# Eight fixed PSUM banks in rings, in place of banks that the framework hands out

## The chip, the cores and the metric

The kernel runs on one core of one Trainium2 chip. The metric is device time in microseconds. The unchanged kernel takes 2862.86 us, the median of three runs (2862.85 to 2863.44). TensorE (PE) multiplies matrices and writes the sums to PSUM, a memory of 8 banks; a bank holds 128 partitions of 512 fp32 numbers, one tile of this kernel. VectorE (DVE) and ScalarE (ACT) read the sums out. A bank may be written again only when its reader is done.

## The reference

The reference computes one step of a two-layer encoder trunk for 1024 frames of a new stream and 32 frames of a running one, width 1024, all in fp32:

```
for layer in range(2):
    h = rmsnorm(x, norm_w[layer])
    x = x + (ssd_mixer(h) if layer == 0 else hgrn_mixer(h))
    x = x + (silu(hn @ w_gate) * (hn @ w_up)) @ w_down      # hn = rmsnorm(x), hidden width 2816
y = rmsnorm(x, final_norm_w)
```

`ssd_mixer` projects to 5152 columns, runs a causal convolution of four taps over 3072 of them and a chunked state-space scan of 32 heads, gates and normalizes the result and projects back. `hgrn_mixer` projects to 4 x 1024, runs a chunked gated linear recurrence of 8 heads of 128 x 128, and projects back. States and the convolution's last rows are outputs too.

## The kernel before

The frames stand in the free dimension and are worked on in two halves: half 0 has 512 frames and half 1 has 512 + 32, which matmuls take in two blocks of 272. Features stand on the partitions, so a product of a 128-column piece of a weight with a half needs 8 steps of 128 for the width 1024. An fp32 product is made of three faster ones: each operand is split into a high part (a copy on ScalarE in a shorter format, `wh`, `fh`, `xn`) and the rest (a subtraction on VectorE, `wl`, `fl`), and `product` issues high x high (L344), high x low (L345) and low x high (L346) into one PSUM tile.

The work runs in this order: statistic and normalization of x; the SSD projections, convolution and scan, both halves; its output projection; FFN 1, half 0 then half 1; the HGRN mixer; FFN 2; the final norm. Four groups of products matter here:

- `psum_mm` tiles hold dense products: the projections, the FFN's gate, up and down products. `psum_sc` tiles hold the rest: transposes, the small products of the scans, and the sum over features of a norm's statistic (`rstd_of`, L367 and L365).
- The FFN's hidden units are made partly by `ffn_unit`, which combines inputs and weights before multiplying so that fewer products are needed (`part`, L1103 to L1105), with tiles `px`, `py`, `pz`. `ffn_outs` then multiplies a slab of hidden units by the down weights (an "out") and `accumulate` has VectorE add each result to the running sum, a fixed tile (`fixed<-mm,fixed` in the profile).
- In the SSD mixer, `ssd_cols` transposes the packed time steps `dt` four times for a half (L540), each followed by a copy on VectorE (L541).
- In the HGRN mixer, each of 16 head units runs chunks: a score product (L884), two transposes (L888, L889) that ScalarE copies to `hkv`, a state product (L899) and an output product (L901, L903).
- `last_outs` is the last stretch: the down products of the last two slabs of FFN 2, half 1 (L1381), with the final norm between them. Its tiles come from `psum_mm((0, 1))`.

Many functions are lifted: the framework's scheduler sets the order of instructions on each engine from priorities and data dependencies, among them when a PSUM tile is free. Before the change a product asks the pool `pm` for a tile by a tag, `mm0` to `mm4` or `sc`. In the built program tiles of every tag lie in all eight banks: the framework assigns them.

## Time and profile before

| | |
|---|---|
| median of 3 runs | 2862.86 us |
| the profiled execution's own time | 2863.26 us |
| its span (first to last instruction) | 2861.5 us |
| busy: TensorE, VectorE, ScalarE | 2830.7, 2139.4, 1571.6 us |
| mean granted TensorE clock | 0.999 |
| matmuls in the profile | 19676 |

A group's busy time is the sum of its durations; matmuls are pipelined, so one that is shown with 0.40 us follows the one before after 0.23 us. "idle before <-releaser" in a row of the timeline is the time in which its engine had nothing to do, and what ended it. A window's row lists, after its length, the busy time of TensorE, of its weight loads, of VectorE, ScalarE and GpSimd, each with its count, then the granted clock, the share of DMA time and GB/s.

### The profile page before, as it was taken

The numbers are of one execution on the slowest core, as the hardware profiler recorded it, in microseconds if no ns is written. First come the engines' busy times: TensorE is split into PE (matmuls) and PEld (weight loads), VectorE is DVE, ScalarE is ACT, GpSimd is POOL, SyncE is SP. The second block draws the span as 40 slices with busy tenths as digits, with TensorE's granted clock in tenths as the row PEclk, the third lists the DMA queues.
The fourth block names the chain that finished last, engine by engine and source line by source line (L and its number), as shares of the span: only waits on it lengthen the run. The fifth ranks groups of instructions, "written<-read, shape, count | busy, mean of one in ns | idle before, by whom it ended". The sixth has DMA issues, their size and how long they took to land.

```text
span 2861.5 us, 48969 instructions
## 1 busy us (share of the span) xinstructions
PE 2830.7 (99%) x19676; PEld 2608.2 (91%) x19676; DVE 2139.4 (75%) x3712; ACT 1571.6 (55%) x2926; POOL 40.8 (1%) x157
## 2 busy tenths in 40 slices
PE   8999999999999999999999999999999999999998
PEld 7777788999979999999999888999988999999998
DVE  7887887787787877797777566556658877787776
ACT  6665654564644644465444567656544644455544
POOL 0000000000100000000000000000000000000000
PEclk9999999999999999999999999999999999999999
DMA  6443334444322332323333222222222332333322
GB/s 183 114 114 110 95 101 111 115 112 106 104 79 89 118 103 91 111 90 97 96 97 105 59 76 83 79 80 73 80 83 89 119 96 89 120 93 109 109 91 69
DMA packets 394518, 281.56 MB, mean 98 GB/s; under 512 B 16289, under 2 KB 382514, under 8 KB 394290
## 3 DMA queue, kind: packets, MB, share of 16 engines
q1 hardware_dynamic: 394274, 278.42, 33.5%
q8 instruction: 154, 2.52, 0.4%
q14 instruction: 74, 0.61, 0.1%
q10 hardware_dynamic: 16, 0.00, 0.0%
HBM read 270.57 MB, written 7.82 MB: 97 GB/s over the span
## 4 chain that ended last, share of the span: by engine, by line
PE 91%; DVE 5%; ACT 2%; issue 1%; DMA 0%; SPq 0%; POOL 0%; DVEq 0%; ACTq 0%; POOLq 0%
PE mm L344 18%; PE mm L345 18%; PE mm L346 18%; PE mm L1105 5%; PE mm L1103 5%; PE mm L1104 5%; PE sc L1105 4%; PE sc L1104 4%; PE sc L1103 4%; PE sc L659 1%; PE sc L648 1%; PE sc L645 1%; PE mm L1381 1%; DVE fixed L116 1%; DVE ca L119 1%
## 5 line engine op out<-in xcount | busy, mean ns | idle before, releaser
L113 ACT ACTIVATE wh<-raw 128x512 fp32r<-128x512 f32 (+1 forms) x687 | 555.1, 817 | 616.5 <-PE mm L345 510.5
L344 PE MATMUL mm<-xn,wh 128*128 128x272 f32 (+2 forms) x1552 | 523.3, 338 | 5.1 <-ACT wh L113 2.1
L346 PE MATMUL mm<-xn,wl 128*128 128x272 f32 (+2 forms) x1552 | 517.9, 334 | 1.7 <-DVE wl L116 1.7
L345 PE MATMUL mm<-xn,wh 128*128 128x272 f32 (+2 forms) x1552 | 516.9, 333 | 0.0
L116 DVE TENSOR_TENSOR wl<-raw,wh 128x1024 fp32r<-128x1024 f32 (+1 forms) x307 | 372.6, 1216 | 80.2 <-ACT wh L113 61.0
L116 DVE TENSOR_TENSOR fixed<-mm,fixed 128x272 f32<-128x272 f32 (+3 forms) x504 | 259.0, 524 | 193.1 <-PE mm L346 186.6
L344 PEld LDWEIGHTS mm<-xn,wh 128*128 128x128 f32 x1552 | 291.6, 188 | 35.4 <-ACT wh L113 3.1
L344 PE MATMUL mm<-fh,wh 128*128 128x272 f32 (+1 forms) x992 | 322.5, 327 | 0.3 <-ACT fh L113 0.3
L345 PE MATMUL mm<-fl,wh 128*128 128x272 f32 (+1 forms) x992 | 322.5, 326 | 0.0
L346 PE MATMUL mm<-fh,wl 128*128 128x272 f32 (+1 forms) x992 | 322.4, 326 | 0.0
L346 PEld LDWEIGHTS mm<-xn,wl 128*128 128x128 f32 x1552 | 291.6, 188 | 30.4 <-DVE wl L116 2.1
L345 PEld LDWEIGHTS mm<-xn,wh 128*128 128x128 f32 x1552 | 292.0, 188 | 27.2 <-issue 1.0
L116 DVE TENSOR_TENSOR wh<-raw,wh 128x512 fp32r<-128x512 f32 x380 | 255.6, 684 | 39.8 <-ACT wh L113 36.9
L1103 PE MATMUL mm<-th,wh 128*128 128x272 f32 (+1 forms) x912 | 260.7, 286 | 0.7 <-ACT s L113 0.7
L1105 PE MATMUL mm<-th,wh 128*128 128x272 f32 (+1 forms) x912 | 259.9, 285 | 0.2 <-DVE wh L116 0.2
L1104 PE MATMUL mm<-tl,wh 128*128 128x272 f32 (+1 forms) x912 | 259.7, 285 | 0.0
L344 PEld LDWEIGHTS mm<-fh,wh 128*128 128x128 f32 x992 | 186.2, 188 | 16.9 <-ACT fh L113 1.9
L346 PEld LDWEIGHTS mm<-fh,wl 128*128 128x128 f32 x992 | 186.6, 188 | 15.5
L345 PEld LDWEIGHTS mm<-fl,wh 128*128 128x128 f32 x992 | 186.6, 188 | 15.0 <-DVE fl L116 0.2
L1103 PEld LDWEIGHTS mm<-th,wh 128*128 128x128 f32 x912 | 171.8, 188 | 2.5 <-ACT s L113 1.8
L1104 PE MATMUL sc<-xn,wh 128*128 128x272 f32 (+1 forms) x608 | 173.3, 285 | 0.0
L1103 PE MATMUL sc<-xn,wh 128*128 128x272 f32 (+1 forms) x608 | 172.9, 284 | 0.0
(289 smaller groups left out, 6712.9 us busy)
## 6 DMA issues: line engine op xcount, KB each, us to landing
raw<-in_ffn_w_gate_dram SPq DMA_DIRECT2D x88, 512.0 KB, 3.8
raw<-in_ffn_w_up_dram SPq DMA_DIRECT2D x88, 512.0 KB, 3.9
raw<-in_ffn_w_down_dram SPq DMA_DIRECT2D x88, 512.0 KB, 3.5
raw<-in_ssd_in_w_dram SPq DMA_DIRECT2D x80, 512.0 KB, 4.0
raw<-in_hgrn_in_w_dram SPq DMA_DIRECT2D x64, 512.0 KB, 4.2
cumB<-cumd SPq DMA_DIRECT2D x64, 256.0 KB, 5.3
raw<-in_ssd_out_w_dram SPq DMA_DIRECT2D x32, 512.0 KB, 5.3
raw<-in_hgrn_out_w_dram SPq DMA_DIRECT2D x16, 512.0 KB, 3.8
```

The source lines that it names most:

```text
L113: keep(A.activation(out=out, in_=in_, func=f, **kw))
L116: keep((eng or V).tensor_tensor(out=out, in0=a, in1=b, op=op))
L119: keep(V.scalar_tensor_tensor(out=out, in0=a, scalar=s, in1=b, op0=op0, op1=op1))
L344: PE.matmul(ps[:, :bn], a, mh, start=(k == 0), stop=False)
L345: PE.matmul(ps[:, :bn], a, ml, start=False, stop=False)
L346: PE.matmul(ps[:, :bn], b, mh, start=False, stop=(k == n - 1))
L645: PE.matmul(y23[:, j, :n], S[:, j * P:(j + 1) * P], Cx, start=True, stop=True)
L648: PE.matmul(pp, Btok[:n, :], xw[:n, :], start=True, stop=True)
L659: PE.matmul(y13[r:r + 64, i // 2, :n], xdt[:n, i * 64:(i + 1) * 64], cums[i // 4][:n, i % 4, :n], start=True, stop=True)
L1103: PE.matmul(ps[:, :n], a, mh, start=(k == 0 and not more), stop=False, skip_group_check=True)
L1104: PE.matmul(ps[:, :n], a, ml, start=False, stop=False, skip_group_check=True)
L1105: PE.matmul(ps[:, :n], b, mh, start=False, stop=(k == 3), skip_group_check=True)
```

## The change

Eight PSUM tiles are made once, one for each bank, and kept: `mm0` to `mm3` in banks 0 to 3 and `sc4` to `sc7` in banks 4 to 7. Every kind of product has a tuple of banks, and each tuple has a counter that moves by one with each request in the order in which the code is issued. Dense products take 0, 1, 2, 3; scans, transposes and statistics 4, 5, 6, 7; the FFN's outs, the final norm's transposes and the statistics inside an FFN half take 2, 3, 4; `px` takes 0, 1 as before, `py` and `pz` 5, 6, 7; `last_outs` 0, 1. The three matmuls, the copies, the DMAs and their numbers stay. Lines of the profile after the change lie 3 later up to about line 1008 and 6 later behind it (L344 becomes L347, L1381 becomes L1387).

```diff
-    turn = [0]
-
-    def psum_mm(among=(0, 1, 2, 3, 4)):
-        turn[0] += 1
-        i = among[turn[0] % len(among)]
-        return pm.tile([P, 512], F32, tag=f"mm{i}", bufs=1, name=nm("mm"))
+    banks = [pm.tile([P, 512], F32, tag=f"bank{i}", bufs=1, name=f"{'mm' if i < 4 else 'sc'}{i}") for i in range(8)]
+    turns = {}
+
+    def psum(among):
+        turns[among] = turns.get(among, -1) + 1
+        return banks[among[turns[among] % len(among)]]
+
+    def psum_mm(among=(0, 1, 2, 3)):
+        return psum(among)
 
     def psum_sc():
-        return pm.tile([P, 512], F32, tag="sc", bufs=3, name=nm("sc"))
+        return psum((4, 5, 6, 7))
...
-    def rstd_of(tiles, blocks, scale, width, keep=None, halves=False):
+    def rstd_of(tiles, blocks, scale, width, keep=None, halves=False, bank=psum_sc):
...
-            ps = psum_sc()
+            ps = bank()
...
+    def psum_outs():
+        return psum((2, 3, 4))
...
-        py, pz = psum_sc(), psum_sc()
+        py, pz = psum((5, 6, 7)), psum((5, 6, 7))
...
-            ps = psum_mm((2, 3, 4))
+            ps = psum_outs()
             product(ps, ws[c], (m * P) % cols, hid, b0, bn)
             accumulate(h, m, ps, b0, bn)
...
-        due = ffn_half(layer, 0, xn[0], tx[0], HEAD, lambda: r.append(x_stat(1, st[2])), [2])
+        due = ffn_half(layer, 0, xn[0], tx[0], HEAD, lambda: r.append(x_stat(1, st[2], psum_outs)), [2])
```

Three places of TensorE's order show what this moves. A row is a line, an operation, the tile it writes, the tiles it reads and the shape; before, every request has a tile of its own with a number of its own, while after the change the name is the bank.

The tail, `last_outs`, before: the first three products of the last slabs, `mm_4776`, `mm_4777` and `mm_4778`, and the last product of an FFN unit, `mm_4741`, between them.

```order
L1381 MATMUL mm_4776_30752<-fh_4733_30505,wh_4766_30732 128x288
...
L1105 MATMUL mm_4741_30552<-th_4275_26916,wh_4757_30698 128x272
L1381 MATMUL mm_4776_30752<-fl_4736_30511,wh_4766_30732 128x288
L1381 MATMUL mm_4776_30752<-fh_4735_30510,wl_4767_30733 128x288
L1381 MATMUL mm_4777_30760<-fh_4733_30505,wh_4766_30732 128x288
...
L1381 MATMUL mm_4778_30768<-fh_4733_30505,wh_4766_30732 128x288
```

The same rows after:

```order
L1387 MATMUL mm0_72<-fh_3164_28944,wh_3194_29168 128x288
...
L1111 MATMUL mm1_73<-th_2842_25491,wh_3185_29134 128x272
L1387 MATMUL mm0_72<-fl_3167_28950,wh_3194_29168 128x288
L1387 MATMUL mm0_72<-fh_3166_28949,wl_3195_29169 128x288
L1387 MATMUL mm1_73<-fh_3164_28944,wh_3194_29168 128x288
...
L1387 MATMUL mm0_72<-fh_3164_28944,wh_3194_29168 128x288
```

Nothing has moved; the third product now writes the bank of the first.

The outs of the first slabs of FFN 1, half 0, about 840 us into the span, before: the last matmuls of the SSD output projection, the statistic (L367) between transposes of the final SSD state (L584), and the first matmul of each of five outs.

```order
L346 MATMUL mm_1439_8941<-xn_92,wl_1437_8913 128x512
L584 MATMUL sc_1441_8971<-fixed_72 128x128 x4
L584 MATMUL sc_1443_8979<-fixed_72,Ss_1281_7992 128x128
L367 MATMUL sc_1450_9011<-sq_1445_8999,fixed_72 128x272
L584 MATMUL sc_1443_8979<-fixed_72,Ss_1281_7992 128x128 x3
L367 MATMUL sc_1451_9014<-sq_1445_8999,fixed_72 128x272
L344 MATMUL mm_1463_9044<-fh_1409_8784,wh_1461_9040 128x512
...
L344 MATMUL mm_1464_9052<-fh_1409_8784,wh_1461_9040 128x512
...
L344 MATMUL mm_1465_9060<-fh_1409_8784,wh_1461_9040 128x512
...
L344 MATMUL mm_1466_9068<-fh_1409_8784,wh_1461_9040 128x512
...
L344 MATMUL mm_1470_9082<-fh_1409_8784,wh_1468_9078 128x512
```

After:

```order
L370 MATMUL sc5_77<-sq_957_8519,fixed_80 128x272
L370 MATMUL sc6_78<-sq_957_8519,fixed_80 128x272
L348 MATMUL mm2_74<-xn_100,wh_952_8436 128x512
L349 MATMUL mm2_74<-xn_100,wl_953_8437 128x512
L587 MATMUL sc7_79<-fixed_80 128x128 x4
L587 MATMUL sc4_76<-fixed_80,Ss_855_7574 128x128 x4
L347 MATMUL mm3_75<-fh_933_8316,wh_971_8558 128x512
L347 MATMUL mm2_74<-fh_933_8316,wh_971_8558 128x512
...
L347 MATMUL sc4_76<-fh_933_8316,wh_971_8558 128x512
...
L347 MATMUL mm2_74<-fh_933_8316,wh_971_8558 128x512
...
L347 MATMUL mm3_75<-fh_933_8316,wh_974_8592 128x512
```

The statistic now stands ahead of the transposes and of two matmuls of the projection, and the outs go through three banks.

The start of the SSD mixer, some 50 us into the span, before: the end of one convolution product, the first matmul of the next (`mm_82`), and the transposes of dt further on.

```order
L344 MATMUL mm_75_605<-xn_92,wh_71_573 128x256
L345 MATMUL mm_75_605<-xn_92,wh_71_573 128x256
L346 MATMUL mm_75_605<-xn_92,wl_72_574 128x256
L344 MATMUL mm_82_648<-xn_92,wh_79_642 128x256
...
L540 MATMUL sc_96_790<-fixed_72,dt_50_359 128x128
L540 MATMUL sc_97_793<-fixed_72,dt_50_359 128x128
L540 MATMUL sc_98_796<-fixed_72,dt_50_359 128x128
L344 MATMUL mm_107_814<-xn_92,wh_104_809 128x512
```

After:

```order
L347 MATMUL mm2_74<-xn_100,wh_47_557 128x256
L348 MATMUL mm2_74<-xn_100,wh_47_557 128x256
L349 MATMUL mm2_74<-xn_100,wl_48_558 128x256
L543 MATMUL sc7_79<-fixed_80,dt_32_349 128x128
L543 MATMUL sc4_76<-fixed_80,dt_32_349 128x128
L543 MATMUL sc5_77<-fixed_80,dt_32_349 128x128
L543 MATMUL sc6_78<-fixed_80,dt_32_349 128x128
L641 MATMUL sc5_77<-fixed_80,ca_30_341 128x128
L347 MATMUL mm3_75<-xn_100,wh_53_624 128x256
```

The four transposes, 96 rows further on before, stand ahead of the convolution product `mm3` (before, `mm_82`), and behind them a transpose of the first convolved tile, `ca`, into the bank of the third.

More of the change, by code (lines that the diff above doesn't have):

```diff
@@ L1006, in trunk_kernel, with x_stat @@
     NB = 1
-    def x_stat(h, keep):
-        return rstd_of([acc[h][m][:, :LEN[h]] for m in range(KD)], BLK[h], 1.0 / D, LEN[h], keep)
+    def x_stat(h, keep, bank=psum_sc):
+        return rstd_of([acc[h][m][:, :LEN[h]] for m in range(KD)], BLK[h], 1.0 / D, LEN[h], keep, bank=bank)
+    def psum_outs():
+        return psum((2, 3, 4))
     def norm_pieces(h, wc, out, blocks, r, tags=XN, keep=None):
@@ L1288, in mixer_ffn @@
                 dma(wrow[q], final_norm_w[q * 512:(q + 1) * 512].unsqueeze(0).to_broadcast([P, 512]))
-            done = [lambda g=g: finish(g, lambda: psum_mm((2, 3, 4))) for g in groups_of(0, 0, H1)]
-        due = ffn_half(layer, 1, xn[1], tx[1], 1, lambda: r.append(nxt and x_stat(0, st[3])),
+            done = [lambda g=g: finish(g, psum_outs) for g in groups_of(0, 0, H1)]
+        due = ffn_half(layer, 1, xn[1], tx[1], 1, lambda: r.append(nxt and x_stat(0, st[3], psum_outs)),
                        [2] if nxt else [1, 1], done)
@@ L1342, in first @@
             for g, ss in zip(groups, sums):
-                ps, yo = finish_half(g, 0, ss, lambda: psum_mm((2, 3, 4)), "n")
+                ps, yo = finish_half(g, 0, ss, psum_outs, "n")
                 tt(yo[:g[2], :], ps[:g[2], :], wrow[0][:g[2], :], MUL)
```

## The prediction

> **What bounds the kernel now.** I read the page first, then the list of what TensorE waits for, then single stretches of the timeline.
>
> ```profile
> span 2861.5 us, 48969 instructions
> PE 2830.7 (99%) x19676; PEld 2608.2 (91%) x19676; DVE 2139.4 (75%) x3712; ACT 1571.6 (55%) x2926; POOL 40.8 (1%) x157
> PEclk9999999999999999999999999999999999999999
> PE 91%; DVE 5%; ACT 2%; issue 1%; DMA 0%; SPq 0%; POOL 0%; DVEq 0%; ACTq 0%; POOLq 0%
> ```
>
> TensorE is busy 2830.7 of 2861.5 us and makes 91% of the chain of waits. All its idle time is 2861.5 - 2830.7 = 30.8 us, so no arrangement of banks can gain more than that, while a new wait of TensorE goes into the time one for one. The list of its waits (engine, tile and line that waits, then what it waits for; total, times, longest) says which part of the idle time is about banks:
>
> ```profile
> PE mm L210 <- DMA fixed<-in_x_prompt_dram: 4.2, 1, 4.2
> PE sc L899 <- ACT hkv L113: 2.2, 2, 1.2
> PE mm L344 <- DVE fixed L886: 2.0, 2, 1.7
> PE mm L344 <- DVE fixed L116: 1.3, 1, 1.3
> PE mm L344 <- ACT pre L113: 1.3, 2, 0.8
> PE mm L344 <- DVE hq L119: 0.8, 1, 0.8
> ```
>
> A first matmul of a product (L344) that waits for the engine reading an older product waits for its bank: rows three to six, 2.0 + 1.3 + 1.3 + 0.8 = 5.4 us. The others wait for operands. So what banks cost today is about 5.4 us of 2861.5, and what is to be weighed is what three or four banks per kind add.
>
> **The change part by part.** No matmul, copy or DMA is added or removed. Every bank must be emptied by its reader before the ring comes round to it. The cost at a place is the time at which VectorE or ScalarE has read the bank, less the time at which TensorE would write it again; both can be read from the trace wherever the order stays as it is. The order is the same around 850 to 1500, 2100 to 2500 and 2500 us to the end but for a few rows, and differs in the first 165 us, in 350 to 460, 700 to 850 and 1500 to 2110 us.
>
> *The tail* (`last_outs`, L1381). The first rows are TensorE's, the others VectorE's.
>
> ```profile
> 2825.99 0.41 PE L1381 MATMUL mm<-fh,wh 128*128 128x288 f32 x1 [0.26 <-ACT fxd L113]
> 2826.90 0.30 PE L1381 MATMUL mm<-fh,wh 128*128 128x288 f32 x1
> ...
> 2825.81 1.22 DVE L116 TENSOR_TENSOR wl<-raw,wh 128x1024 fp32r<-128x1024 f32 x1
> 2828.78 0.72 DVE L116 TENSOR_TENSOR fl<-fxd,fh 128x544 fp32r<-128x544 f32 x1
> 2829.42 3.00 DVE L116 TENSOR_TENSOR fixed<-mm,fixed 128x288 f32<-128x288 f32 x8
> ```
>
> The second and third of these product groups begin at 2825.99 and 2826.90. VectorE works through low halves of weights (from 2825.81) and of the hidden rows (2828.78) and reaches the first accumulate at 2829.42. Today the groups run on into other banks. With banks 0 and 1 alone the third group writes the bank of the first, so it starts when that accumulate ends, one of eight accumulates later, at 2829.42 + 3.00 / 8 = 2829.8, or a little after: **+3.0 us**. Afterwards a group takes 0.9 us of TensorE (2825.99 to 2826.90) against 0.4 of an accumulate, and nothing more is lost. Nothing behind can hide it: the rest of the span is this chain.
>
> *The first outs of FFN 1* (512 columns, ring of banks 2, 3, 4).
>
> ```profile
> 846.59 0.40 PE L344 MATMUL mm<-fh,wh 128*128 128x512 f32 x1
> ...
> 846.31 2.18 DVE L119 SCALAR_TENSOR_TENSOR Y<-Y,fixed,rstd 128x544 f32<-128x544 f32 x3 [1.28 <-ACT rstd L113]
> 850.37 1.88 DVE L116 TENSOR_TENSOR fixed<-mm,fixed 128x512 f32<-128x512 f32 x3
> ```
>
> The fourth out starts at 846.59. The first three accumulates come at 850.37, behind the gating of the SSD output that VectorE does in order; the first ends a third into them and a little later, at 851.05. With three banks the fourth out waits for it: 851.05 - 846.59 = 4.4 us. The change also puts the statistic that releases VectorE (1.28 us of waiting for `rstd`) some 1.3 us earlier in TensorE's order. VectorE can come earlier by no more than that wait, so the ends are 4.4 - 1.28 = 3.1 and 4.4; I take **+3.2**.
>
> *Three more places of outs.* After slab 4 of the same FFN, and at the head of the second half of each FFN, where VectorE makes the input combinations (`xt`, `tl`) between the accumulates:
>
> ```profile
> 907.61 0.40 PE L344 MATMUL mm<-fh,wh 128*128 128x512 f32 x1
> ...
> 908.70 0.68 DVE L116 TENSOR_TENSOR fixed<-mm,fixed 128x512 f32<-128x512 f32 x1
> ...
> 2506.81 0.29 PE L344 MATMUL mm<-fh,wh 128*128 128x272 f32 x1
> ...
> 2508.01 1.13 DVE L116 TENSOR_TENSOR fixed<-mm,fixed 128x272 f32<-128x272 f32 x3
> 2500.00:2520.00 20.00, 19.84 (x154) 19.29 (x153) 19.08 (x42) 8.43 (x17) 0.00 (x0) 1.00 0.09 27
> ```
>
> The sixth out (907.61) needs the third accumulate (908.70 + 0.68 = 909.38): 1.8, of which I give back 0.8 for short waits that stand there today: **+1.0**. The seventh out at 2506.81 needs the fourth accumulate, first of the three at 2508.01, ended at 2508.44: 1.6, and in the next groups up to 2.1. VectorE is busy 19.08 of these 20 us (third number pair of the row), so it can't catch up: **+1.8**. The same stretch of FFN 1 at 1216 to 1231 us has the same instructions with VectorE a little freer: **+1.3**.
>
> *The start of the SSD mixer.* The four transposes of dt (L540) and a transpose behind them (L638) are moved in front of a convolution product.
>
> ```profile
> 50.45 0.28 PE L344 MATMUL mm<-xn,wh 128*128 128x256 f32 x1
> 59.85 0.38 PE L344 MATMUL mm<-xn,wh 128*128 128x256 f32 x1 [0.79 <-ACT pre L113]
> 65.23 0.33 PE L540 MATMUL sc<-fixed,dt 128*128 128x128 f32 x1 [1.05 <-ACT pre L113]
> ...
> 52.63 0.68 DVE L116 TENSOR_TENSOR dt<-dt,dt 32x512 f32<-32x512 f32 x1
> 53.35 0.75 DVE L119 SCALAR_TENSOR_TENSOR ca<-pre,fixed,ca 128x512 f32<-128x512 f32 x1
> 65.54 0.88 DVE L541 COPY fixed<-sc 128x128 f32<-128x128 f32 x4
> ```
>
> TensorE is at that product at 50.45; dt is ready at 52.63 + 0.68 = 53.31, and the extra transpose writes the bank of the third of the four, whose copy comes after `ca` (53.35 + 0.75) and three copies of 0.22: about 54.8. That is 4.3 us of standing. Queued behind it on TensorE is the convolution product, and behind that ScalarE's `pre`. The waits of 0.79 and 1.05 us at 59.85 and 65.23 go: **+2.4**; ends 0 and 4.3.
>
> *HGRN mixer* (1590 to 2110 us, 16 head units). Its four small products per chunk share banks 4 to 7, and the statistic takes one of them, so that twice in a unit a bank comes round early: the transposes (L888, L889) of the next unit follow the last ones in the same bank with one product and three 512 or 272 wide matmuls between, about 0.7 us from write to write.
>
> ```profile
> 1593.97 0.27 PE L889 MATMUL sc<-fixed,hv 128*128 128x128 f32 x1
> 1594.28 0.39 ACT L113 ACTIVATE hkv<-sc 128x256 f32<-128x256 f32 x1 [0.51 <-PE sc L889]
> 1600.60 0.27 PE L889 MATMUL sc<-fixed,hv 128*128 128x128 f32 x1
> 1602.73 0.37 ACT L113 ACTIVATE hkv<-sc 128x256 f32<-128x256 f32 x1
> ```
>
> The copy that frees the bank is done 1594.28 + 0.39 - 1593.97 = 0.70 us after the write where ScalarE stands ready, and 2.5 us after it where ScalarE is busy (1600.60, 1602.73). So a place costs 0 or up to 1.8. Of 32 places I let a quarter cost half of that, 32 x 0.25 x 0.9 = 7, take back the 2.0 + 0.8 us of L886 and `hq` waits, and one more for places that hide each other: **+3**; ends -5 and +11. Outside the mixer half of the two 1.3 us waits should go: **-1**. The rest of the reordered rows, at the start and in 700 to 835 us, I take as 0, give or take 3, since TensorE's queue there is dense in both orders.
>
> Sum: 3.0 + 3.2 + 1.0 + 1.8 + 1.3 + 2.4 + 3 - 1 = 14.7 us. Against the profiled execution's own 2863.26 us, which lies 0.4 above the median of 2862.86, that is **2878 us**, or +0.5%.
>
> [...]
>
> **The rivals.**
>
> *Gain.* Banks that are free by rule end the bank waits of today, and the new order feeds TensorE better: the statistic at 840 us and the dt transposes already move forward. Of the 30.8 us of idle time 4.2 is the wait for x; if half of the rest goes and the outs hide, only the tail adding its 3.0, it gives 2863.3 - 13.3 + 3.0 = 2853, within 2850 and 2859. Against it: the 5.4 us of bank waits is all that I could find for certain.
>
> *Absorbed.* While TensorE stands, VectorE and ScalarE catch up, so that a stall early on pays for a later one, and only the tail remains, with half of the outs' 7.3 us, less some 3 us of bank waits that go: 3.0 + 3.6 - 3 gives 2867. For it: VectorE has a quarter of the span free. Against it: at 2500 to 2520 it has not.
>
> *Compounding.* The mixer's short turns cost their 11 us and the SSD start is not regained (4.3): 14.7 + 8 + 2 = +25, 2888.
>
> [...]
>
> *The change doesn't do what it says.* The framework might already keep tags to banks, and the rings would then be nearly the old ones. The built order speaks against it: products that the code tags alike lie in all eight banks before. It would give 2863.
>
> **How the numbers follow.** The forecast holds 0.50, compounding 0.13, the clock 0.05, absorbed 0.16, nothing done 0.03, gain 0.13. A measurement of this kernel can tell about 0.2% from no change, 5.7 us: below 2857.1 is faster, above 2868.6 slower. Of the gain rival 0.11 lies below 2857 and 0.02 within; of the absorbed one 0.12 within and 0.04 above; nothing done lies within. So faster has 0.11, no change 0.12 + 0.03 + 0.02 = 0.17, and slower 0.50 + 0.13 + 0.05 + 0.04 = 0.72. The range leaves out one in ten on either side: low 2858, where the gain begins; high 2892, past compounding by the 3 us of the unknown reorderings. The forecast's own range is 2870 to 2886.
>
> **What would show it.** The tail: a wait of the `last_outs` matmuls for VectorE's `fixed` of about 3.0 us, and the first accumulate at the same distance from the end of the product as now. The outs: a wait of `product`'s first matmul for VectorE of about 3 us some 846 us in, and waits of 1 to 2 us near 907, 1220 and 2507. The start: one of the dt transposes waiting about 2.9 us for `dt`, then the extra one 1.4 us for `fixed`. The mixer: transposes into a `sc` bank waiting for ScalarE's `hkv`, ten or so, none above 2 us. [...] I am wrong if the outs and the tail show no wait for VectorE, if VectorE's own order of accumulates is earlier than now, or if the waits are there and the time isn't because as much idle time vanished elsewhere.

## The result

The changed kernel takes 2897.57 us (median of four runs, 2896.24 to 2899.33) against 2863.15 us (2862.85 to 2863.5) for the kernel before: a ratio of 1.0121, with a 95% interval of 1.0103 to 1.0138. It is slower, as forecast, but by 34.4 us and not by 14.7, and outside the range of 2858 to 2892.

The page of the changed kernel, with the rows that answer to those shown of before (its profiled execution took 2899.33 us):

```profile
span 2897.6 us, 48939 instructions
PE 2846.6 (98%) x19676; PEld 2613.9 (90%) x19676; DVE 2141.3 (74%) x3712; ACT 1574.8 (54%) x2926; POOL 56.8 (2%) x157
PE 88%; DVE 7%; ACT 3%; DMA 1%; issue 1%; SPq 1%; POOL 0%; DVEq 0%; ACTq 0%; POOLq 0%
```

The span is 36.1 us longer. TensorE's idle time has grown from 30.8 to 51.0 us, but its busy time has grown too, by 15.9 us, with the same 19676 matmuls. So waits are not the whole story: some matmuls have become slower. The list of what TensorE waits for, its first rows:

```profile
PE mm L347 <- DVE fixed L119: 8.1, 11, 2.2
PE mm L213 <- DMA fixed<-in_x_prompt_dram: 4.6, 2, 4.2
PE sc L543 <- DVE dt L119: 3.0, 1, 3.0
PE mm L1387 <- DVE fixed L119: 2.9, 1, 2.9
PE mm L349 <- DVE wl L119: 2.4, 3, 0.9
PE sc L620 <- DVE ca L122: 2.3, 1, 2.3
```

The first row is the outs waiting for their accumulates, the fourth is the tail, the third the dt transposes at the start of the SSD mixer; all three were forecast. The second row, the wait for x, stood before the change too (4.2 us). The last two rows are small: the fifth stood before with 1.7 us, and the sixth was not forecast. Rows of the timeline of TensorE in the changed kernel say when the longest ones came:

```profile
55.09 1.11 PE L543 MATMUL sc<-fixed,dt 128*128 128x128 f32 x4 [3.03 <-DVE dt L119]
...
429.62 0.28 PE L543 MATMUL sc<-fixed,dt 128*32 128x128 f32 x1 [1.93 <-DVE fixed L544]
...
747.55 1.13 PE L370 MATMUL sc<-sq,fixed 128*128 128x512 f32 x2 [1.69 <-ACT fixed L116]
751.01 0.49 PE L620 MATMUL sc<-ca,ca 128*128 128x128 f32 x2 [2.34 <-DVE ca L122]
...
866.84 0.50 PE L347 MATMUL mm<-fh,wh 128*128 128x512 f32 x1 [2.15 <-DVE fixed L119]
...
2861.05 0.61 PE L1387 MATMUL mm<-fh,wh 128*128 128x288 f32 x1 [2.88 <-DVE fixed L119]
```

And the windows right behind five of them (length, TensorE's busy time and count, ..., granted clock, DMA share, GB/s):

```profile
55.00:62.00 7.00, 6.65 (x29) 6.09 (x30) 5.48 (x11) 4.35 (x12) 0.73 (x2) 0.51 1.05 274
430.00:434.00 4.00, 4.00 (x20) 3.84 (x20) 3.96 (x7) 4.00 (x13) 2.81 (x4) 0.57 0.69 212
751.00:755.00 4.00, 3.98 (x20) 3.99 (x21) 2.44 (x5) 3.86 (x8) 0.57 (x2) 0.57 0.70 188
867.00:871.00 4.00, 4.00 (x11) 3.17 (x12) 2.80 (x4) 1.60 (x2) 0.00 (x0) 0.57 0.23 70
2861.00:2865.00 4.00, 3.95 (x19) 3.95 (x20) 1.27 (x3) 0.00 (x0) 0.00 (x0) 0.60 0.00 0
```

The granted clock is 0.51 to 0.60 where it is 1.00 in the kernel before. The records of the clock in this trace have it at half for 6.83 us from 55 us on and for 3.41 us behind each of the other four, 6.83 + 4 x 3.41 = 20.5 us together; if TensorE does half of its work there, that is 20.5 / 2, some 10 of the 36.1 us by my estimate.

**Where the 36 us are.** To compare two kernels whose order differs, I took the time at which TensorE has issued the same amount of work in both, counting each matmul with its interval in dense stretches (0.232 us for 512 columns, 0.125 for 272, 0.118 for 256). The table has how much the lead of the kernel before grows in each stretch, in us (stretches in its own time), from each kernel's profiled execution; e3 to e12 are the experiments below.

| stretch | what runs there | forecast | changed | e3 | e4 | e5 | e6 | e7 | e9 | e12 |
|---|---|---|---|---|---|---|---|---|---|---|
| 0-140 | norm, SSD start | 2.4 | 5.6 | 6.9 | 18.1 | 4.2 | 6.6 | 6.8 | 0.4 | 20.0 |
| 140-400 | SSD, half 0 | 0 | 1.8 | 1.1 | 0.4 | 1.3 | 0.7 | 0.7 | 1.0 | -1.5 |
| 400-440 | dt of half 1 | 0 | 2.6 | 2.4 | 0.1 | 2.8 | 2.6 | 3.4 | -0.4 | 0.4 |
| 440-730 | SSD, half 1 | 0 | 0.1 | 0.5 | 3.3 | 0.7 | 2.3 | 0.3 | 3.9 | 0.9 |
| 730-810 | last SSD group | 0 | 7.3 | 7.2 | 6.8 | 8.2 | 9.6 | 7.0 | 2.1 | 4.2 |
| 810-960 | first outs, FFN 1 half 0 | 4.2 | 5.8 | 1.7 | 4.7 | 7.4 | 5.2 | 4.8 | 3.9 | 3.2 |
| 960-1570 | rest of FFN 1 | 1.3 | 1.7 | 0.4 | 2.2 | 1.9 | 0.7 | 1.1 | 0.2 | 2.0 |
| 1570-2145 | HGRN mixer | 3 | 1.4 | 6.0 | 3.0 | 3.6 | -0.8 | 2.7 | 11.3 | 2.7 |
| 2145-2290 | first outs, FFN 2 half 0 | 0 | 3.1 | 0.6 | 1.2 | 0.5 | 1.1 | 2.1 | 1.3 | 1.5 |
| 2290-2800 | rest of FFN 2 | 1.8 | 1.5 | 1.6 | 1.5 | 1.0 | 1.3 | 1.2 | 1.0 | 1.1 |
| 2800-end | tail | 3.0 | 5.0 | 1.5 | 5.3 | 3.3 | 5.1 | 5.1 | 4.8 | 1.8 |

The places where the working was done from rows (outs, HGRN mixer, tail) come out near it. Ten of the missing 20 us stand in rows that the prediction took as nought: 2.6 at 400 to 440 and 7.3 at 730 to 810. Some 3 us of these are half clock (the falls behind 430 and 751 us), so this count and the 10 us of half clock overlap.

### The profile page after: what moved, and what is told of

The parts are those of the page before. It is cut to its first block, busy times and chain, and to the rows that moved or that the text cites. A ratio compares the mean times of both kernels' runs of the same rounds, so it can differ in the third digit from the quotient of the medians.

```text
span 2897.6 us, 48939 instructions
## 1 busy us (share of the span) xinstructions
PE 2846.6 (98%) x19676; PEld 2613.9 (90%) x19676; DVE 2141.3 (74%) x3712; ACT 1574.8 (54%) x2926; POOL 56.8 (2%) x157
## 4 chain that ended last, share of the span: by engine, by line
PE 88%; DVE 7%; ACT 3%; DMA 1%; issue 1%; SPq 1%; POOL 0%; DVEq 0%; ACTq 0%; POOLq 0%
PE mm L347 17%; PE mm L348 16%; PE mm L349 16%; PE mm L1111 5%; PE mm L1109 5%; PE mm L1110 5%; PE sc L1111 4%; PE sc L1110 4%; PE sc L1109 4%; PE sc L347 2%; PE sc L348 2%; PE sc L349 2%; PE sc L662 1%; PE sc L651 1%; PE sc L648 1%
## 5 line engine op out<-in xcount | busy, mean ns | idle before, releaser
L347 PE MATMUL mm<-xn,wh 128*128 128x272 f32 (+2 forms) x1552 | 526.6, 340 | 3.0 <-ACT pre L116 1.6
L119 DVE TENSOR_TENSOR fixed<-mm,fixed 128x272 f32<-128x272 f32 (+3 forms) x408 | 209.6, 521 | 160.8 <-PE mm L349 150.3
L347 PEld LDWEIGHTS mm<-xn,wh 128*128 128x128 f32 x1552 | 294.3, 190 | 33.4 <-issue 3.5
L347 PE MATMUL mm<-fh,wh 128*128 128x272 f32 (+1 forms) x660 | 216.4, 329 | 7.6 <-DVE fixed L119 7.0
L348 PE MATMUL mm<-fl,wh 128*128 128x272 f32 (+1 forms) x660 | 215.2, 326 | 0.6 <-DVE fl L119 0.6
L349 PE MATMUL mm<-fh,wl 128*128 128x272 f32 (+1 forms) x660 | 215.1, 326 | 0.0
L1109 PEld LDWEIGHTS mm<-th,wh 128*128 128x128 f32 x912 | 171.7, 188 | 1.7 <-ACT s L116 1.2
L1110 PE MATMUL sc<-xn,wh 128*128 128x272 f32 (+1 forms) x608 | 173.1, 285 | 0.0
L1111 PE MATMUL sc<-xn,wh 128*128 128x272 f32 (+1 forms) x608 | 172.8, 284 | 0.0
L1109 PE MATMUL sc<-xn,wh 128*128 128x272 f32 (+1 forms) x608 | 172.6, 284 | 0.0
L1110 PEld LDWEIGHTS mm<-tl,wh 128*128 128x128 f32 x912 | 171.8, 188 | 0.6 <-issue 0.2
L1111 PEld LDWEIGHTS mm<-th,wh 128*128 128x128 f32 x912 | 171.6, 188 | 0.0
```

Source lines behind the costliest of these rows:

```text
L119: keep((eng or V).tensor_tensor(out=out, in0=a, in1=b, op=op))
L347: PE.matmul(ps[:, :bn], a, mh, start=(k == 0), stop=False)
L348: PE.matmul(ps[:, :bn], a, ml, start=False, stop=False)
L349: PE.matmul(ps[:, :bn], b, mh, start=False, stop=(k == n - 1))
L1109: PE.matmul(ps[:, :n], a, mh, start=(k == 0 and not more), stop=False, skip_group_check=True)
L1110: PE.matmul(ps[:, :n], a, ml, start=False, stop=False, skip_group_check=True)
```

## The experiments

Each kernel is the changed one with a small edit, unless it says otherwise. The two questions are whether the half clock is charged to the waits, and why the SSD mixer lost so much.

### e1 and e2: a wider ring for the tail

```diff
         def out(m, groups, b0, bn):
-            ps = psum_mm((0, 1))
+            ps = psum((0, 1, 2, 3, 4))        # e1; (0, 1, 2) in e2
```

> Only last_outs differs from the changed kernel: it goes through banks 0 to 4 in place of 0 and 1. Theory A (a wait of TensorE beyond some 2 us is followed by about 3.4 us at half clock, so it costs itself and 1.7 us more): the wait of 2.9 us for the first accumulate goes, and the digit below full clock behind it goes too; from the first matmul of last_outs to the end 4.7 us less, 2893 in all. Rival (the low clock in the records costs nothing, the wait alone does): 3.0 us less, 2894.5. Rival (VectorE is the bound of the tail, so the wait only moves to a later group): under 1 us less.

> As before this but with banks 0, 1 and 2 for last_outs. One more group fits ahead of the first accumulate, so the wait is 2.9 - 0.9 = 2.0 to 2.1 us. Theory A: if 2.1 us is beyond the clock's bound (2.1 us at 429 us was followed by half clock, 1.9 us at 747 was not) the tail is 0.9 us shorter than in the changed kernel, and if not 2.6 us shorter. Rival (clock costs nothing): 0.9 us shorter either way.

e1 took 2893.96 us, 3.6 less than the changed kernel, e2 2896.82. TensorE's rows in e1 and in e2, and the window behind each:

```profile
2858.99 0.40 PE L1387 MATMUL mm<-fh,wh 128*128 128x288 f32 x1 [1.01 <-DVE fixed L119]
...
2858.00:2865.00 7.00, 6.01 (x45) 6.01 (x46) 5.20 (x13) 0.00 (x0) 0.00 (x0) 1.00 0.01 2
```

```profile
2859.39 0.40 PE L1387 MATMUL mm<-fh,wh 128*128 128x288 f32 x1 [2.61 <-DVE fixed L119]
...
2859.00:2865.00 6.00, 5.61 (x30) 5.61 (x31) 2.89 (x7) 0.00 (x0) 0.00 (x0) 0.72 0.01 3
```

With five banks the wait is 1.0 us and the clock stays; the stretch from 2800 on loses 1.7 us against the kernel before and not 5.0. So 3.3 us came back, not 4.7: a later group waits 1.0 us where I had none, which is most of what is missing. Three banks leave a wait of 2.6 us, more than the 2.0 to 2.1 that I expected, the clock still falls, and only 0.8 us come back. Going from 2.9 to 2.6 us of wait gives 0.8; from 2.6 to 1.0 gives 2.5. The second step is 0.9 us more than the wait alone, which speaks for the clock, but not cleanly.

These two kernels gave a cleaner pair by chance. At 430 us nothing is edited. The window there in e1, then in e2:

```profile
430.00:434.00 4.00, 4.00 (x32) 3.84 (x32) 3.96 (x8) 4.00 (x13) 2.80 (x4) 1.00 0.61 174
```

```profile
430.00:434.00 4.00, 4.00 (x20) 3.84 (x20) 3.96 (x7) 4.00 (x13) 2.80 (x4) 0.57 0.70 228
```

The same instructions, ahead of them the same standing still of 1.88 us, and in e2 the clock falls, in e1 it doesn't: 20 matmuls in 4 us against 32. The stretch of 400 to 440 us loses 2.6 us with the fall (e2 and the changed kernel) and 1.1 without it. So a fall costs 1.5 us there, and at 1.9 us of standing it may come or not.

### e8: keep TensorE busy in the tail's wait

```diff
         for g in (g1, g2):
             for m in range(KD):
                 out(m, [g], 256, LEN[h] - 256)
+                if g is g1 and m == 1:
+                    for i in range(14):
+                        a, x = next(terms(w1, 0, hid1))[0]
+                        PE.matmul(banks[2][:, :288], a, x[:, 256:544], start=True, stop=True)
```

> The changed kernel with 14 matmuls more, of 0.133 us each, into a bank that nobody reads at that time, ahead of the third product of last_outs. They fill 1.9 us of TensorE's wait of 2.9 us there; the wait for the accumulate ends when it did. Theory A (the clock falls after a long wait): what is left of the wait is 1.2 to 1.5 us, the clock stays at full, and the end comes 1.7 us earlier although work was added. Rival (the low clock in the records costs nothing): no change. Rival (added work costs its time): 1.9 us later.

TensorE's rows of the added matmuls and of the product that waits, and the window:

```profile
2854.01 0.69 PE L1397 MATMUL mm<-fh,wh 128*128 128x288 f32 x4
2855.35 1.49 PE L1397 MATMUL mm<-fh,wh 128*128 128x288 f32 x10
2858.37 0.40 PE L1387 MATMUL mm<-fh,wh 128*128 128x288 f32 x1 [1.53 <-DVE fixed L119]
...
2858.00:2865.00 7.00, 6.63 (x49) 6.63 (x50) 3.88 (x9) 0.00 (x0) 0.00 (x0) 1.00 0.01 2
```

The ring is still two banks, and the product still starts when VectorE's accumulate is done. Only the standing still is shorter, 1.5 us, and the clock stays at 1.00. From the first product of `last_outs` to the end the kernel needs 42.0 us against 43.4 of the changed kernel, although 14 matmuls were added (38.5 before). Adding work made the tail 43.4 - 42.0 = 1.4 us shorter; with the wait's end fixed by VectorE, that leaves the clock (1.00 in this window, 0.60 behind the whole wait in the changed kernel). That filling the wait kept the clock up is argued from this one execution: in e5, further on, it is 1.00 behind the whole wait too. The whole took 2893.94 us, 3.6 less than the changed kernel, but that is not all the tail's: in its profiled execution e8 also loses only 0.3 us at 2145 to 2290 us, where the changed kernel loses 3.1 and nothing was edited.

### e3 and e5: one half of the rings fixed

In e3 the dense products, outs, px and the tail get four banks from the framework, and 4 to 7 stay rings:

```diff
-    banks = [pm.tile([P, 512], F32, tag=f"bank{i}", bufs=1, name=f"{'mm' if i < 4 else 'sc'}{i}") for i in range(8)]
+    banks = [None] * 4 + [pm.tile([P, 512], F32, tag=f"bank{i}", bufs=1, name=f"sc{i}") for i in range(4, 8)]
...
-    def psum_mm(among=(0, 1, 2, 3)):
-        return psum(among)
+    def psum_mm(among=None):
+        return pm.tile([P, 512], F32, tag="mm", bufs=4, name=nm("mm"))
...
-        return psum((2, 3, 4))
+        return psum_mm()
```

> Banks 4 to 7 stay fixed rings for scans, transposes, statistics, py and pz; all dense products, the outs, px and last_outs get the other four banks from the framework. Theory A (narrow rings make the scheduler put other work ahead, which then waits for operands): in the built order the dt transposes at 50 us are back at their place behind the convolution, so the first 140 us lose under 1.5 us and not 5.4; those at 430 us and the pulled-forward products at 747 us stay, so 705 to 790 us still loses about 9. With four banks the outs at 866 us and the tail wait 1 to 1.5 us less per place and the clock stays up: 5.5 to about 2 and 5.0 to about 1.5. In all about 2884. Rival B (products bound to the order of issue, whatever the number of banks, is the cause): the start is as slow as in the changed kernel, 2890 or more, since sc is still bound.

e3 took 2893.52 us. The outs and the tail answered as expected: 1.7 and 0.6 us at the first outs of the two FFNs (5.8 and 3.1 in the changed kernel) and 1.5 us in the tail. 730 to 810 us stayed, 7.2. But 12.9 us were lost in two other stretches: 6.9 at the start, where a transpose waits 4.0 us for a VectorE copy, and 6.0 in the HGRN mixer, where transposes wait for `hk`. That the start would be cured was wrong: the dt transposes are back behind the convolution, and something else stands. By its numbers rival B came true (a slow start, 2890 us or more), but e9 below speaks against its reason, a binding whatever the width. And 730 to 810 us is as slow with four dense banks that the framework hands out as with four in a ring.

In e5 it is the other way round: banks 0 to 4 are rings, and the rest gets three banks from the framework.

```diff
-    ... for i in range(8)]
+    ... for i in range(5)]
...
     def psum_sc():
-        return psum((4, 5, 6, 7))
+        return pm.tile([P, 512], F32, tag="sc", bufs=3, name=nm("sc"))
...
-        py, pz = psum((5, 6, 7)), psum((5, 6, 7))
+        py, pz = psum_sc(), psum_sc()
```

> The other half of e3: banks 0 to 4 stay fixed rings for dense products, the outs, px and last_outs; scans, transposes, statistics, py and pz get the other three banks from the framework. Theory A2 (a ring taken in the order of issue makes a product wait for all that was issued ahead of it in its ring, so the scheduler, which lifts statistics and chunks, pulls their predecessors forward too; each kind's ring acts at its own places): in the built order the pulled-forward products at 747 us are back behind the convolutions, so 730 to 770 us loses under 1 us and not 8.3; the dt transposes at 55 and 430 us stay forward (4.4 and 1.1 to 2.6), the outs and the tail stay (4.3, 1.4, 1.1, 1 to 3, 1.0, 5.0). In all about 2889. Rival (width alone): sc with three banks in place of four is worse, 2900 or more.

e5 took 2900.13 us (two runs, 2897.95 and 2902.3). The products that were pulled forward at 747 us are back behind the convolutions in its order, and 730 to 810 us still loses 8.2 us. My theory of a pulled-forward order fails here for the first time: in that stretch TensorE now waits 4.0 us for ScalarE's `pre`. The rival's 2900 us lie between the two runs, so that the whole decides nothing; three banks cost the HGRN mixer 3.6 us here against 1.4.

e5 also has the tail's two banks, as the changed kernel has. Its product there and the window behind:

```profile
2861.38 0.40 PE L1387 MATMUL mm<-fh,wh 128*128 128x288 f32 x1 [2.87 <-DVE fixed L119]
...
2861.00:2865.00 4.00, 3.62 (x27) 3.62 (x28) 2.17 (x6) 0.00 (x0) 0.00 (x0) 1.00 0.00 0
```

The wait is the same (2.87 us; 2.88 in the changed kernel), and the clock did not fall. The tail lost 3.3 us and not 5.0. That is the forecast's 3.0 us for the wait alone, and 1.7 us for the clock, with nothing else different there. It also shows that 2.9 us of standing do not always bring the fall.

### e6 and e7: put the moved products back, one at a time

```diff
-    def rstd_of(tiles, blocks, scale, width, keep=None, halves=False, bank=psum_sc):
+    def rstd_of(tiles, blocks, scale, width, keep=None, halves=False, bank=psum_mm):   # e6 alone
...
         for c, (o, n, _) in enumerate(CHUNKS[h]):
-            ps = psum_sc()
+            ps = psum_mm()                                                              # e7 alone
             PE.transpose(ps[:n, :P], pk[:, o:o + n], ident)
```

> One line of the changed kernel: the statistics of the norms take their bank from the ring of the dense products (0 to 3) in place of 4 to 7. The lifted statistic then no longer pulls the chunk's transpose and products forward at 747 us; the built order has the statistic 224 rows later. A2: 730 to 770 us loses under 2 us and not 8.3, of which 1.7 is clock; the rest is as in the changed kernel, in all 2890. Rival (that stretch is slow because VectorE is late with the squares and ca whatever the order): 730 to 770 still loses 6 or more.

> One line of the changed kernel: the dt transposes take their bank from the ring of the dense products. In the built order they are back behind the convolutions at both halves. A2: 30 to 70 us loses about 1 us and not 4.4, 400 to 440 us under 0.5 and not 1.1 to 2.6; the rest as in the changed kernel: about 2891. Rival (the convolution product there stands for its own bank, so TensorE only waits for something else): both stretches stay within 1 us of the changed kernel's.

They took 2896.34 and 2897.11 us, and the stretches concerned did not get better: 9.6 at 730 to 810 us in e6, 6.8 up to 140 us and 3.4 at 400 to 440 us in e7. TensorE's timeline in e6, then in e7 with two rows of ScalarE's ahead of the wait's end:

```profile
752.27 0.59 PE L347 MATMUL mm<-xn,wh 128*128 128x272 f32 x1 [4.35 <-ACT pre L116]
```

```profile
56.55 0.58 PE L347 MATMUL mm<-xn,wh 128*128 128x256 f32 x1 [4.62 <-ACT pre L116]
...
55.59 0.63 ACT L116 ACTIVATE cth<-ca 128x512 f32<-128x512 f32 x1 [1.91 <-DVE ca L122]
56.13 0.64 ACT L116 ACTIVATE pre<-mm 128x256 f32<-128x256 f32 x2
```

The rivals were right. With the moved products out of the way TensorE stands at the same place for as long, now for `pre`: the copy by which ScalarE reads a convolution product out of its bank. It is late because ScalarE first does the tanh of the tile before (`cth`), which waits for VectorE's convolution sums (`ca`). In the kernel before, which is 1.2 us ahead of e7 there, these copies come about as late (ScalarE's rows):

```profile
54.13 0.63 ACT L113 ACTIVATE cth<-ca 128x512 f32<-128x512 f32 x1 [1.90 <-DVE ca L119]
54.67 0.64 ACT L113 ACTIVATE pre<-mm 128x256 f32<-128x256 f32 x2
```

There TensorE waited only 0.8 us for `pre`, at 59.85: it had gone on into other banks meanwhile. A ring of four holds four such products. So the moved transposes seem only to have filled a time in which the dense ring was full, when the scheduler had nothing else to give to TensorE; e9 puts that to the test.

### e9 and e10: one bank more for the dense ring

```diff
-    def psum_mm(among=(0, 1, 2, 3)):
+    def psum_mm(among=(0, 1, 2, 3, 4)):
...
     def psum_sc():
-        return psum((4, 5, 6, 7))
+        return psum((5, 6, 7))
```

> The changed kernel with the default ring of dense products one bank wider (0 to 4) and that of scans, transposes and statistics one narrower (5 to 7); outs, px, py, pz and last_outs as changed. Theory A3, formed after e6 and e7, where the moved products were back and TensorE then waited 4.4 to 4.6 us for the pre copy of an older convolution product: in the SSD stage the reader of the dense ring is late, since pre stands behind the tanh of the convolution in ScalarE's queue, which waits for VectorE; a ring of four holds two blocks of 272 columns of two tiles, and a fifth bank is 2.8 to 3.0 us more of slack. So 30 to 70 us loses under 1.5 us (4.4 in the changed kernel), 400 to 440 under 0.5 (2.6), 730 to 770 under 1.5 (8.3), with no half clock there; the outs and the tail stay (about 17 us), three banks for sc cost the HGRN mixer 1 to 4 us. In all 2880 to 2886. Rival (binding to the order of issue, whatever the width): within 3 us of the changed kernel, 2895 or more.

> e9 and e1 together: last_outs goes through banks 0 to 4 as well. If the places are independent, e9's time less 3.3 to 3.7 us (what e1 took from the tail). If a stall of the one paid for one of the other, less than 2 us.

e9 took 2892.93 us (2892.09 to 2894.06, ratio 1.0104, interval 1.0091 to 1.0118), e10 2888.09. The dense ring is the cause in the SSD mixer: 0 to 140 us loses 0.4 us, 400 to 440 gains 0.4, and 730 to 810 loses 2.1, with the order of the kernel before at all three places although nothing was done about the order. e9 also narrows the other ring, but e5 had three banks there too and cured nothing. The fifth bank doesn't take the wait for `pre` away altogether: 2.1 us of it are left at 55 us, and 1.5 us at 730 to 810. And the total missed the upper end of what I expected by 7 us; this shows where. TensorE's waits in e9 in the HGRN mixer, 1590 to 2150 us, then those of the changed kernel there:

```profile
PE sc L887 <- ACT hkv L116: 4.5, 5, 1.2
PE sc L891 <- DVE fixed L119: 3.6, 5, 1.7
PE sc L902 <- ACT ho L116: 1.0, 1, 1.0
```

```profile
PE sc L891 <- DVE hk L119: 1.3, 2, 1.1
PE sc L891 <- ACT hkv L116: 1.1, 1, 1.1
PE sc L891 <- DVE fixed L848: 1.0, 1, 1.0
```

With three banks for scans and transposes the mixer waits 9.1 us in these three rows, and the stretch loses 11.3 us and not 1.4. That is what the prediction feared of four banks (its upper end was 11). The bank moved from one kind to the other earned 5.2 + 3.0 + 5.2 = 13.4 us at those three places and cost 11.3 - 1.4 = 9.9 in the HGRN mixer and 3.8 more in the SSD's half 1, so that the two sides cancel. That e9 is faster than the changed kernel lies in the other stretches (1.9 us at 810 to 960, 1.5 at 960 to 1570 and 1.8 at 2145 to 2290 by the table), which no run takes apart. e10 is 4.8 us below e9, where e1 was 3.6 below the changed kernel: the tail's loss is its own. The 1.2 us beyond it lie near the 1.6 us by which 810 to 960 us differs (3.9 us lost in e9, 2.3 in e10): behind the same wait of 2.23 us there the granted clock was 0.66 in e9 (858 to 863 us) and 1.00 in e10 (859 to 864 us).

### e4 and e12: banks shared between kinds

e4 takes the products that ask `psum_mm` and `psum_sc` for any bank from one ring of eight, while the outs, `px`, `py`, `pz` and the tail keep theirs; e12 gives the convolution's products a ring of six, two of which the chunks use as well, and the tail five.

```diff
-    def psum_mm(among=(0, 1, 2, 3)):
+    def psum_mm(among=tuple(range(8))):               # e4
...
-        return psum((4, 5, 6, 7))
+        return psum(tuple(range(8)))                  # e4
...
         for (b0, bn) in blocks:
-            ps = psum_mm()
+            ps = psum((0, 1, 2, 3, 4, 5))             # e12, in conv_tile; last_outs as in e1
```

> All tiles stay fixed and are taken in the order of issue, but psum_mm and psum_sc share one ring of all eight banks; the rings of px, py, pz, the outs and last_outs stay as changed. Theory A (the width of the rings): order around 50, 430 and 747 us as in the kernel before; 0 to 140 us and 705 to 790 us lose nothing, the HGRN mixer at most 1; the outs (5.5 + 1.2 + 1.3 + 3.0 + 1.0 us by place) and the tail (5.0) stay: 2863 + 17 = 2880. Rival B (the order of issue): as slow as the changed kernel in the mixers, 2895 or more. Rival C (bank waits alone, the moved order is harmless): the mixers differ little from the changed kernel, 2893 or more.

> The changed kernel with two rings wider: the convolution's products alone take banks 0 to 5, last_outs takes 0 to 4; all else as changed, so scans and transposes keep four banks. A3 (the reader of the convolution's products is late, and only they need the width): 30 to 70 us loses under 1.5 us, 400 to 440 under 0.5, 730 to 770 under 2, as in e9, and the HGRN mixer stays at the 1.4 us of the changed kernel and not e9's 11; the tail 1.5; the outs as changed, 9 to 11. In all 2876 to 2881. Rival (banks 4 and 5 shared with the chunks make these wait as long as the convolution did): 2888 or more.

Both expectations were wrong, and the times are those of the rivals: 2910.37 us and 2900.67 us (ratio 1.0132, interval 1.0117 to 1.0148). At 400 to 440 us both lose little (0.1 and 0.4 us), but 0 to 140 us loses 18 and 20 us. Half of e4's 18 is lost in the first 20 us, where transposes of x wait 8.1 us for their data (4.2 before); 14.5 of e12's 20 are lost between 100 and 140 us. The waits of e4 at 770 to 830 us, then those of e12 at 70 to 150 us:

```profile
PE mm L347 <- DVE z L122: 4.7, 1, 4.7
PE sc L347 <- ACT fixed L116: 2.0, 1, 2.0
```

```profile
PE sc L213 <- DVE fixed L226: 5.9, 2, 4.1
```

In a ring that several kinds share, each product waits for whichever kind comes next in the ring, however late its reader: a product of the output projection (L347) for VectorE's reader of a gate product (`z`) one round of the ring earlier, a transpose of x (L213) for a copy on VectorE that stands behind other work. So neither narrow rings for each kind nor a wide one for all gives back what the framework's free choice had. That this is because it takes the bank that is free when the product is ready to go is argued; no run here changed the framework's choice alone.

### e11 and e13: a busy TensorE at the start, in the kernel before

```diff
+    ps = psum_mm()
+    for i in range(12):                               # 7 in e13
+        PE.matmul(ps[:, :P], ones, ones, start=True, stop=True)
     in_order[0] = True
     rows = norm_rows()
```

> The kernel before with 12 fp32 matmuls of 128 columns more at its start, on a constant tile, into a bank that is not read, while TensorE waits 4.2 us for x. In the kernel before the transposes that follow take 0.24 us each at 4 to 14 us and 0.11 later, though the record of the clock begins later and shows none of it. If this is the half clock of a TensorE that has just begun, the transposes at 4 us or at the latest those at 9 us take 0.11 us, up to 2.7 us are won at 15 us, and what is left after the wait for weights is 0 to 2.5 us of the whole: 2860.5 to 2863. Rival (the transposes are slow because of their operands): they stay at 0.24 us and the time is the same.

> As e11, but with 7 matmuls in place of 12: in e11 the 12 took until 6.2 us, 2 us longer than the wait for x, at half pace for most of it, and the first dense product started 1.5 us earlier than in the kernel before. With 7 they end at about 4.3 us. If the clock has risen by then or during the first transposes, the first dense product starts at 13.0 to 13.5 us, 3 us earlier than before, and the whole is 2860.0 to 2861.0, clear of the kernel before. If 3 us of work are too few to raise the clock, the transposes at 4 us stay slow and those at 9 us are fast or not: 2861 to 2863.

The first 12 transposes of x and the first 12 of the norm (L402), in the kernel before, in e11 and in e13:

```profile
4.18 2.95 PE L210 MATMUL mm<-fixed 128*128 128x128 f32 x12 [4.18 <-DMA fixed<-in_x_prompt_dram]
8.87 2.93 PE L402 MATMUL sc<-fixed 128*128 128x128 f32 x12 [1.54 <-DVE fixed L383]
```

```profile
6.20 1.47 PE L210 MATMUL mm<-fixed 128*128 128x128 f32 x12
...
9.37 1.60 PE L402 MATMUL sc<-fixed 128*128 128x128 f32 x12 [1.54 <-DVE fixed L383]
```

```profile
8.44 2.93 PE L402 MATMUL sc<-fixed 128*128 128x128 f32 x12 [1.54 <-DVE fixed L383]
```

The same 12 transposes take 2.95 us in the kernel before, as TensorE's first work, and 1.47 us in e11, behind 5.24 us of other matmuls: at the start of the kernel before TensorE ran at half pace. The page shows full clock for that kernel, but the clock's record in its trace begins only at 13.84 us, behind these transposes; the durations are what tells. In e11 the second dozen takes 1.60 us, near full pace too. Seven matmuls (3.35 us) were enough for the transposes of x: in e13 they take 0.63 to 0.67 us for four, against 0.60 for four at 15.06 us and 1.06 at 11.16. But the second dozen takes 2.93 us there, half pace again, behind waits of 0.22 and 0.29 us for x and of 1.54 us for VectorE. The times are 2861.18 us against 2863.26 (ratio 0.9995, interval 0.9986 to 1.0004) and 2862.04 against 2863.2 (0.9997, 0.9988 to 1.0006): neither can be told from the kernel before. No version that was run is clear of it on the fast side.

## Why the prediction was right in sign and wrong in size

**What bounds the kernel, and the direction:** right. The chain still is TensorE's (88%), and the waits for readers went into the time, some of them with more than their length. The 5.4 us of bank waits could indeed not pay for the new ones.

**The tail, 3.0 us:** the wait was 2.88 us, at the place and for the reason that was given, but the stretch lost 5.0. The term left out the half clock behind the wait (0.60 from 2861 to 2865 us; in e5, where it stayed at 1.00, the stretch lost 3.3). The 0.26 us that TensorE waits there in the kernel before is a wait for an operand (`fxd`), and stands after the change too (0.27 us).

**The outs, 3.2 + 1.0 + 1.3 + 1.8 us:** mostly right. 810 to 960 us lost 5.8 where 4.2 was said: the wait for the accumulate at 866.84 us was 2.15 us, and 0.72 us came on top for a bank of the ring that the last state transposes had just written, read by ScalarE (`so`). The two waits that the prediction placed near 907 us came at 926 and 930 us, 0.52 + 0.73 = 1.25 us; the rest, 1.7 us, is what 3.41 us at half clock come to (0.57 from 867 to 871 us). The heads of the half-1 FFNs lost 1.1 and 1.0 us where 1.3 and 1.8 was said. The same place in FFN 2, half 0 (2264 us) was not looked at: 1.7 us of wait there, and 3.1 us lost in this execution, though 0.3 to 2.4 in e1, e2 and e8 with the same instructions. The difference lies in a weight that comes late to VectorE, whose accumulates stand behind it. VectorE's row in the changed kernel:

```profile
2261.68 0.69 DVE L119 TENSOR_TENSOR fixed<-raw,raw 128x512 f32<-128x512 f32 x1 [3.59 <-DMA raw<-in_ffn_w_gate_dram]
```

This wait is 3.59 us in the changed kernel, 2.81 in e1 and 1.78 in e2, and what the stretch loses is 3.1, 2.4 and 1.3: the wait less 0.4 to 0.5 us each time. In e8, where the stretch loses 0.3, TensorE doesn't wait from 2263 to 2267 us, nor at that place in the kernel before, where VectorE's wait is 0.52 us.

**The start of the SSD mixer, 2.4 us:** the wait for dt came as worked out (3.03 us; 2.9 said), and the clock fell for 6.83 us behind it; the extra transpose waited 0.27 us and not the 1.4 that was said. Of the 5.6 us lost up to 140 us, 1.5 are lost ahead of 50 us already, where transposes of x that are moved forward wait 2.2 us for their data; this was not reckoned with. But the reason was not seen whole: e7 shows that the transposes stood where TensorE would have stood anyway, for `pre`. Putting them back gains nothing; a fifth bank does (e9).

**"The rest of the reordered rows ... I take as 0, give or take 3, since TensorE's queue there is dense in both orders":** this step failed. TensorE's queue was not dense there: it stood 1.93 us at 430 us and 1.69 + 2.34 us around 750, and 400 to 440 and 730 to 810 us lost 9.9 us, about 3 of them by the half clock behind these waits. The prediction compared, place by place, a bank's last read with its next write for the outs, the HGRN mixer and the tail, where the order was the same or the gaps short, and not for the convolution products, whose reader's delay (`pre` behind `cth` behind `ca`) stands in ScalarE's timeline of the kernel before (the two rows under e7: the tanh waits 1.90 us for `ca`, and `pre` comes behind it). At 400 to 440 us it also missed that five dt transposes go through a ring of four.

**The HGRN mixer, +3 us, ends -5 and +11:** 1.4 us lost, inside the ends, but with luck: ten or so waits for `hkv` were forecast, and there is one, of 1.1 us (rows under e9). e9 shows that the upper end is what three banks cost.

**The relief, -1 us:** 960 to 1570 us shows none that can be told from the outs there.

**The clock (chance 0.05):** it fell, on top of the forecast, at five places, behind waits of 1.93 to 3.03 us (0.51 to 0.60 in the windows above), and cost some 10 us by my estimate. The window of the first 10 us of the kernel before, in which TensorE waits 4.18 us for x, shows 1.00 (third number from the end):

```profile
0.00:10.00 10.00, 4.28 (x18) 3.45 (x19) 2.59 (x25) 4.18 (x9) 2.15 (x11) 1.00 0.81 218
```

That is not full clock: the clock's record begins only at 13.84 us, while the transposes in this window, which I had not timed, ran at half pace (2.95 us for 12). That was in the profile of before.

**Gain, compounding and absorbed:** none of them. TensorE's idle time grew by 20.2 us. Dense stretches between the places run at the same pace in both kernels (0.1 us in 440 to 730), so nothing is given back and nothing spreads. Of compounding's two terms the mixer's 11 us did not come; the start lost more than its 4.3 us, but with the clock and the wait for x in it.

**That the change doesn't do what it says:** it does. That a wide or shared ring would be better was tried and is false for the two that were run (e4, e12).

At 140 to 400 us 1.1 of the 1.8 us are two more waits for accumulates, 0.87 and 0.24 us, of the SSD output projection of half 0 (148.90 and 162.47 us), which the prediction did not look at. What stays open: the other 0.7 us there, what makes the weight at 2260 us come early or late, and where e9's gain in the FFN comes from. The stretches of the table are single executions, so that differences of some tenths between its columns mean nothing.

## What to carry to other kernels

Where a memory is handed out when a product is ready, fixing it into rings by kind and issue order is not a change of names: for each kind, set the time from a bank's last write to its reader's end, in the reader's own queue order, against the time in which the ring comes round, at every stage and not only where the order is unchanged. A reader that stands behind another engine's late work (here a copy behind a tanh behind VectorE) needs the width, and a bank given to one stage is taken from another, so an uneven load wants a common free set. And in this kernel a wait of TensorE of 1.9 to 2.9 us cost 1.4 to 1.7 us on top where the clock fell behind it, a term to set beside the wait itself; in the tail, where nothing else was to be done, 14 unused matmuls in the wait came out 1.4 us cheaper (e8).

## What the runs showed of the hardware

In the changed kernel the granted clock fell to half at five places, for 6.83 us at 55 us and for 3.41 us at each of the other four, behind waits of TensorE of 1.93 to 3.03 us. Why the fall at 55 us lasts longer is not shown. Three comparisons put 3.41 us of it at 1.4 to 1.7 us (e8, 430 us in e1 and e2, the tail in e5).

The same wait had the fall behind it in one execution and not in another: 1.88 us at 430 us did in e2 (0.57 in the window) and not in e1 (1.00), 2.9 us in the tail did in the changed kernel (0.60) and not in e5 (1.00), and 2.23 us at 858 us did in e9 (0.66) and not in e10 (1.00). So the length of the wait alone doesn't decide; what does is not shown here.

With fourteen unread matmuls in the tail's wait 1.53 us of it were left, and the clock was 1.00 behind it (e8). At the start of the program TensorE ran at half pace in the kernel before, 2.95 / 12 = 0.246 us for a transpose of 128 columns, against 1.47 / 12 = 0.123 in e11, behind 5.24 us of other matmuls. The page's clock row doesn't show it, since the record of the clock begins only at 13.84 us there.
